# Two tiles of modulation weights for every three projections, instead of one for every two, in a two-layer mLSTM, RWKV-7 and attention trunk

## The chip, the cores and the metric

The kernel runs on one core of a Trainium2 chip. The core has five engines, each with its own queue that is worked off in order: TensorE (PE) for matmuls into PSUM, VectorE (DVE), ScalarE (ACT), GpSimd (POOL), and SyncE (SP), whose queue here does nothing but wait for semaphores and issue DMAs. The metric is the device time of one execution in microseconds (us); lower is better.

## The reference, cut to what matters

Two layers work on 512 latent and 256 context tokens of width 1024. Before each layer a conditioning vector goes through one large matrix (`ada_w`, 1024 x 6144 for each layer), which gives six modulation vectors: shift, scale and gate for the mixer and for the MLP.

```python
def ada_modulation(cond, w, b):
    m = jax.nn.silu(cond) @ w + b
    return jnp.split(m[:, None, :], 6, axis=-1)
...
for layer in range(DEPTH):
    last = layer == DEPTH - 1
    sx1, cx1, gx1, sx2, cx2, gx2 = ada_modulation(c, ada_w[layer], ada_b[layer])
    sc1, cc1, gc1, sc2, cc2, gc2 = ada_modulation(c_ctx[None], ada_w[layer], ada_b[layer])
    nx = modulate(rms_norm(h_lat), sx1, cx1)
    nc = modulate(rms_norm(h_ctx), sc1, cc1)
    if layer % 2 == 0:
        ox, oc = even_mixer(nx, nc, rope, not last, ev_in_w[e], mix_out_w[layer], ml_gate_b[e], ml_norm_w[e],
...
    else:
        ox, oc = odd_mixer(nx, nc, not last, od_in_w[o], mix_out_w[layer], lru_conv_w[o], lru_conv_b[o],
...
    h_lat = h_lat + gx1 * ox
    h_lat = h_lat + gx2 * sq_relu_mlp(modulate(rms_norm(h_lat), sx2, cx2), mlp_w1[layer], mlp_w2[layer])
    if not last:
        h_ctx = h_ctx + gc1 * oc
        h_ctx = h_ctx + gc2 * sq_relu_mlp(modulate(rms_norm(h_ctx), sc2, cc2), mlp_w1[layer], mlp_w2[layer])
return rms_norm(h_lat) * final_norm_w
```

The even mixer projects its input (`in_w`), runs four mLSTM heads in both directions and eight RWKV-7 heads in both directions, each over the context first and then over the latent tokens, and projects the result out.

## The kernel before, in words

**Projections.** All weights are single precision. `split_w` loads one column block of 128 (0.5 MB) through SP, lets ACT round it to `wh`, and lets POOL or DVE form the rest `wl`. `gemm` then multiplies both halves with the split input, 24 matmuls for each segment of tokens: 512 columns for the latent segment (`psg` 128x512), 256 for the context (128x256). Every matmul carries the line number of the helper `mm` (L134).

**Modulation weights.** `ada` is a generator that works on the matrix `ada_w` in parts. A part takes two tiles `adaw` of 2 MB. A tile is two DMAs of 1 MB each on SP's queue, then 32 rows of small matmuls in the trace (16 in the order of the program, where a single-precision matmul is one row), into `psada`: 16 of them need the first DMA, 16 the second. After the second tile of a part, DVE copies `psada` to `rows` (L172), PE transposes that (`pst`, L175) and DVE writes the columns of `mod` (L184). The tile lives in the pool `pa1` with one buffer: the DMA of a tile waits on SP until the matmuls of the tile before it have read it, and everything behind it in SP's queue waits too. Eight parts are worked off in this way in the stretch of which this document speaks, 16 tiles: four parts of layer 0 (the two gates, and the MLP's shift and scale) and four of layer 1 (the mixer's shift and scale, and the gates). None of these values is used in the stretch itself.

**The mLSTM stretch.** A string of tokens sets the order in which Python emits the program. A digit advances that mLSTM head by one projection (`k`, `q`, `v`, output gate, then the head's recurrence over six chunks of 128: `psn`, `pscn`), `c` advances `rwkv_in(0)`, the input side of RWKV-7 for the context. The token `a` starts the draw of modulation tiles: from there each call of `gemm` adds `bg[1]` to a counter, and each time the counter reaches 1 the next tile of `ada` is emitted. From `a` to the end of the stretch there are 26 calls of `gemm`. At the token `R` the rest of `rwkv_in(0)` and then whatever is left of `ada` are emitted. Then the pool `pa1` is closed, its memory goes to the tiles of the RWKV-7 recurrence, and `pre(0)`, the first step's preparation, is emitted. Head 3's last projection and its recurrence are emitted after that.

**What follows.** `pre(s)` loads `bk` and `ar` of step `s` back from DRAM, where `rwkv_in` put them (`bkD`, `arD`, L803 and L804; loads L849 and L850), multiplies them (`psA`), sends a small part through DRAM to POOL, which inverts a triangular matrix in 30 small operations (`Xi`), sends that through DRAM back (`invD`, `Xr`, L895 and L897) and multiplies again (`psI`). Steps 0 to 11 of the recurrence follow, each with `pre` of the next; projections of `rwkv_in(1)` and the layer's other matmuls are drawn in between as filling.

**What sets the order.** A scheduler of the framework takes the emitted program and lays out each engine's queue at build time, from its own estimates of durations. The queue is then fixed: an engine that comes to an instruction whose input isn't there waits, though later ones could run.

Of the kernel before, what the change touches and what calls it, by code (L numbers as in the profile page):

```python
# [117 lines left out]
def hybrid_kernel(ctx: ExitStack, tc: tile.TileContext, A, out):  # L118
# [4 lines left out]
    def nm(s):  # L123
        uid[0] += 1
        return f"{s}_{uid[0]}"
# [6 lines left out]
    def mm(o, l, r, start=True, stop=True, shared=False, tile=None):  # L132
        kw = {"tile_position": (32 * tile[0], 32 * tile[1])} if tile else {}
        return nc.tensor.matmul(o, l, r, start=start, stop=stop, skip_group_check=shared, **kw)  # L134
# [23 lines left out]
    def ada(layer, parts, pa, psa, tag):  # L158
        for pair, half in parts:
            ps = psa.tile([P, 256], F32, tag=tag, name=nm("psada"))  # L160
            for k0 in range(0, NK, 4):

                w = pa.tile([P, 4, D], F32, tag="adaw", name=nm("adaw"))
                for i in range(0, 4, 2):
                    nc.sync.dma_start(w[:, i:i + 2, :], A["ada_w"][layer, pair, half, (k0 + i) // 2])
                for i in range(4):
                    k = k0 + i
                    for j in range(4):
                        mm(ps[32 * j:32 * j + 32, :], sc[:, k, :], w[:, i, 256 * j:256 * j + 256], k == 0, k == NK - 1)
                yield 1.8  # L170
            rows = pa.tile([P, 256], F32, tag="rows", name=nm("rows"), bufs=1)
            nc.vector.tensor_copy(rows, ps)  # L172
            pt = psa.tile([P, 2, P], F32, tag=tag, name=nm("pst"))
            for t in range(2):
                nc.tensor.transpose(pt[:, t, :], rows[:, P * t:P * t + P], ident)  # L175
            src = pt.rearrange("p t (i j r) -> p i t j r", i=2, j=2)
            for i, idx in enumerate(PAIRS[pair]):
                o = 8 * idx + 4 * half
                dst = mod[:, layer, o:o + 4, :].rearrange("p (j t) c -> p t j c", t=2)
                bo = COLS["ada_b"][0] + 48 * layer + o  # L180
                bias = cols[:, bo:bo + 4].rearrange("p (j t) -> p t j", t=2)
                one = 1.0 if idx in (1, 4) else 0.0
                for cnd in range(2):
                    nc.vector.scalar_tensor_tensor(dst[:, :, :, cnd], src[:, i, :, :, cnd], one, bias, op0=ALU.add, op1=ALU.add)  # L184
# [236 lines left out]
    psa1 = st_p1.enter_context(tc.tile_pool(name="psa1", bufs=1, space=PSUM, side="right"))  # L421
# [53 lines left out]
    pa1 = st_a.enter_context(tc.tile_pool(name="pa1", bufs=1))  # L475
# [348 lines left out]
    def add_set():  # L824

        sets.append(st_r.enter_context(tc.tile_pool(name=f"set{len(sets)}", bufs=1)))
# [119 lines left out]
    def new_x(s):  # L946
        return sets[s % 2].tile([P, 2, 4, 2, 64], F32, tag="X", name=nm("X"))
# [141 lines left out]
    for o in "0000a0c1ccc1cc11c1c22cc2c23c12ccc33cR33":  # L1089
        if o == "a":  # L1090
            bg[:] = [itertools.chain(ada(0, ((1, 0), (1, 1), (2, 0), (2, 1)), pa1, psa1, "ada"),
                                     ada(1, ((0, 0), (0, 1), (1, 0), (1, 1)), pa1, psa1, "ada")), 0.5, 0.0]
        elif o == "R":
            for _ in itertools.chain(work["c"], bg[0]):
                pass
            bg[1] = 0
            st_a.close()
            YA[0] = st_y.enter_context(tc.tile_pool(name="py", bufs=1)).tile([P, 4, 4, 64], F32, name="ya_c")
            pr = st_r.enter_context(tc.tile_pool(name="pr", bufs=1))
            add_set()  # L1100
            banks.update(A=(psh2, "h", 1), I=(psa1, "ada", 1))
            S = sets[0].tile([P, 2, 4, 64], F32, tag="S", name="S0")
            nc.vector.memset(S, 0.0)
            X = new_x(0)
            nc.vector.memset(X[0:64], 0.0)
            pre(0, X)
        else:
            next(work[o], None)
# [376 lines left out]
```

## Time and profile before

| | us |
|---|---|
| median of 3 runs | 2063.24 |
| lowest and highest run | 2058.32, 2063.85 |
| the profiled execution, its own time | 2061.51 |
| its span, first to last instruction | 2059.7 |

The sums below are made against the profiled execution: its own time is 1.81 us longer than its span and 1.73 us below the median of the runs. The profile of this execution shows for each engine when an instruction began and how long it took, and for an instruction that waited what released it, in brackets. PE's ends are modelled, since matmuls overlap: what a row of matmuls costs is read from its start to the start of the next. PEclk is TensorE's granted clock as a share of full speed: 1.00 in a stretch means 2.4 GHz throughout, a matmul that takes nearly twice as long as its neighbours ran at the lower level of 1.2 GHz.

### The profile page before, as it was taken

What the parts mean: (1) busy time and instruction counts of PE and PEld (TensorE: products, weight loads), DVE (VectorE), ACT (ScalarE), POOL (GpSimd) and SP (SyncE); (2) the same over time, 40 slices, a digit from 0 to 9 for tenths busy, and PEclk for the clock granted to TensorE, in tenths of its full rate; (3) what the DMA queues carried; (4) which work ended last, traced back from release to release, by engine and by line L of the source; (5) the groups of instructions that cost most, each with busy time, mean ns of one, the idle gap of its engine ahead of it and who ended that gap; (6) DMA issues with size and microseconds to landing.
All of it is one profiled execution on the core that took longest, in us unless ns stands there. A gap on an engine that the chain in (4) does not pass through costs nothing. (4 is left out here: it accounts for less than half of the span.)

```text
span 2059.7 us, 36771 instructions
## 1 busy us (share of the span) xinstructions
PE 1952.0 (95%) x14924; PEld 1604.6 (78%) x14924; DVE 1055.2 (51%) x1944; ACT 875.5 (43%) x1441; POOL 872.4 (42%) x706
## 2 busy tenths in 40 slices
PE   6899998899887999999999999999999999999998
PEld 4788886777677888988787888888666678888887
DVE  6774645676767666766642221353666664122222
ACT  4444444455534443443432332443655654233232
POOL 1455555445534222223244444435444453444444
PEclk9999999999888999999999999999999999999999
DMA  7356557454585555543533323234211122323332
GB/s 301 107 200 214 178 206 262 122 156 124 153 233 143 159 158 156 142 136 124 190 115 125 102 92 103 88 108 153 62 52 34 57 75 82 102 92 101 94 97 78
DMA packets 171833, 271.62 MB, mean 132 GB/s; under 512 B 74960, under 2 KB 113488, under 8 KB 166544
## 3 DMA queue, kind: packets, MB, share of 16 engines
q1 hardware_dynamic: 166608, 263.76, 40.7%
q10 hardware_dynamic: 5056, 5.51, 0.8%
q8 instruction: 118, 1.93, 0.4%
q14 instruction: 51, 0.42, 0.1%
HBM read 244.06 MB, written 25.17 MB: 131 GB/s over the span
## 5 line engine op out<-in xcount | busy, mean ns | idle before, releaser
L241 POOL TENSOR_TENSOR wl<-w,wh 128x1024 fp32r<-128x1024 f32 (+3 forms) x245 | 555.1, 2268 | 829.1 <-PE psg L134 451.9
L237 ACT CAST wh<-w 128x1024 fp32r<-128x1024 f32 (+3 forms) x319 | 313.5, 985 | 543.5 <-PE psg L134 465.1
L134 PE MATMUL psg<-xh,wh 128*128 128x512 f32 (+1 forms) x1440 | 498.2, 361 | 12.8 <-DVE k L710 3.1
L134 PE MATMUL psg<-xl,wh 128*128 128x512 f32 (+1 forms) x1440 | 497.9, 358 | 0.5 <-DVE xl L335 0.4
L134 PEld LDWEIGHTS psg<-xh,wh 128*128 128x128 f32 x1440 | 273.2, 191 | 68.0 <-issue 16.9
L134 PE MATMUL psg<-xh,wl 128*128 128x512 f32 (+1 forms) x1440 | 325.3, 356 | 0.0
L134 PEld LDWEIGHTS psg<-xl,wh 128*128 128x128 f32 x1440 | 275.4, 191 | 45.0 <-issue 7.2
L134 PEld LDWEIGHTS psg<-xh,wl 128*128 128x128 f32 x1440 | 241.9, 190 | 42.1 <-issue 7.3
L134 PE MATMUL psg<-hh,wh 128*128 128x512 f32 (+1 forms) x800 | 266.9, 350 | 6.2 <-DVE r L383 3.2
L134 PE MATMUL psg<-hl,wh 128*128 128x512 f32 (+1 forms) x800 | 268.8, 350 | 0.9 <-DVE hl L281 0.8
L338 DVE SCALAR_TENSOR_TENSOR res_l<-psg,mod,res_l 128x512 f32<-128x512 f32 (+1 forms) x108 | 74.2, 689 | 276.3 <-PE psg L134 276.2
L134 PEld LDWEIGHTS psg<-hh,wh 128*128 128x128 f32 x800 | 151.9, 190 | 27.6 <-issue 4.2
L134 PEld LDWEIGHTS psg<-hl,wh 128*128 128x128 f32 x800 | 152.1, 190 | 20.6 <-DVE hl L281 1.2
L134 PE MATMUL psg<-hh,wl 128*128 128x512 f32 (+1 forms) x800 | 166.4, 350 | 0.0
L134 PEld LDWEIGHTS psg<-hh,wl 128*128 128x128 f32 x800 | 132.9, 191 | 19.2
L383 DVE TENSOR_SCALAR r<-psg 128x512 f32<-128x512 f32 (+1 forms) x96 | 57.4, 600 | 171.4 <-PE psg L134 171.2
L281 DVE TENSOR_TENSOR hl<-r,hh 128x512 fp32r<-128x512 f32 (+1 forms) x96 | 86.8, 907 | 80.4 <-ACT hh L280 80.4
L384 ACT ACTIVATE r<-r 128x512 f32<-128x512 f32 (+1 forms) x96 | 53.5, 560 | 125.8 <-DVE r L383 125.8
L241 DVE TENSOR_TENSOR wl<-w,wh 128x1024 fp32r<-128x1024 f32 (+1 forms) x74 | 88.1, 1191 | 34.9 <-ACT wh L237 15.5
L134 PE MATMUL psada<-adaw,sc 128*32 128x256 f32 (+1 forms) x896 | 62.4, 383 | 7.7 <-DMA adaw<-in_ada_w_dram 4.1
L134 PE MATMUL psA<-ar,bk 64*128 64x128 f32 x384 | 51.5, 295 | 7.3 <-issue 3.0
L280 ACT CAST hh<-r 128x512 fp32r<-128x512 f32 (+1 forms) x96 | 52.6, 550 | 2.8
(422 smaller groups left out, 2900.5 us busy)
## 6 DMA issues: line engine op xcount, KB each, us to landing
w<-in_w_dram SPq DMA_DIRECT2D x192, 512.0 KB, 3.5
adaw<-in_ada_w_dram SPq DMA_DIRECT2D x40, 1024.0 KB, 7.5
w<-in_ev_in_dram SPq DMA_DIRECT2D x47, 512.0 KB, 3.5
w<-in_od_in_dram SPq DMA_DIRECT2D x32, 512.0 KB, 3.5
adaw<-in_ada_dram SPq DMA_DIRECT2D x16, 512.0 KB, 10.8
w<-in_out_w_dram SPq DMA_DIRECT2D x32, 256.0 KB, 2.9
bk<-bkD SPq DMA_DIRECT2D x12, 512.0 KB, 4.7
ar<-arD SPq DMA_DIRECT2D x12, 512.0 KB, 5.7
```

The lines of the kernel that those rows point to most:

```text
L134: return nc.tensor.matmul(o, l, r, start=start, stop=stop, skip_group_check=shared, **kw)
L237: nc.scalar.copy(wh, w)
L241: eng.tensor_tensor(wl, w, wh.bitcast(F32), op=ALU.subtract)
L280: nc.scalar.copy(h, x)
L281: nc.vector.tensor_tensor(l, x, h.bitcast(F32), op=ALU.subtract)
L338: nc.vector.scalar_tensor_tensor(r_, ps, modcol(layer, idx, m, cnd), r_, op0=ALU.mult, op1=ALU.add)
L383: nc.vector.tensor_scalar(r_, ps, 0.0, None, op0=ALU.max)
L384: nc.scalar.activation(r_, r_, AF.Square)
```

## The change

The counter's step goes from 0.5 to 0.67. Nothing else in the program text differs.

```diff
     for o in "0000a0c1ccc1cc11c1c22cc2c23c12ccc33cR33":
         if o == "a":
             bg[:] = [itertools.chain(ada(0, ((1, 0), (1, 1), (2, 0), (2, 1)), pa1, psa1, "ada"),
-                                     ada(1, ((0, 0), (0, 1), (1, 0), (1, 1)), pa1, psa1, "ada")), 0.5, 0.0]
+                                     ada(1, ((0, 0), (0, 1), (1, 0), (1, 1)), pa1, psa1, "ada")), 0.67, 0.0]
         elif o == "R":
             for _ in itertools.chain(work["c"], bg[0]):
                 pass
```

With 26 calls of `gemm`, 0.5 draws 13 times: 13 tiles are emitted between projections, and at `R` three tiles and the last part's transposes are left. With 0.67 it draws 17 times: all 16 tiles and the last part's transposes are emitted before `R`. The pattern is one projection, two, one, two between draws, where it was always two. The scheduler then lays out the queues anew. Counted in the order of the program, the rows of PE are the same in kind and number; those from the second tile of the stretch to the end of the RWKV-7 recurrence stand in a new order. From the MLP of layer 0 on the order is the same but for a few rows.

The first place is SP's queue at the end of the stretch, where the last modulation tiles stood ahead of the loads of `pre(0)`. Before (`adaw_3605` is the last tile, `w_...` a projection's weights, `bk_3649` and `ar_3648` the first loads of `pre(0)`):

```order
L165 DMA adaw_3605<-in_ada_w_dram 128x2048
L810 DMA vD_580<-vt_3545 128x2x128
L165 DMA adaw_3605<-in_ada_w_dram 128x2048
L235 DMA w_4349<-in_ev_in_dram 128x1024
L803 DMA arD_576<-ar_3529 128x4x128
L804 DMA bkD_578<-bk_3530 128x4x128
L235 DMA w_4391<-in_ev_in_dram 128x1024
L849 DMA bk_3649<-bkD_578 128x1024
L850 DMA ar_3648<-arD_576 128x1024
L852 DMA AS_3651<-arD_576 64x8x64 x2
```

The same place in the changed program:

```order
L810 DMA vD_580<-vt_3621 128x2x128
L235 DMA w_4349<-in_ev_in_dram 128x1024
L803 DMA arD_576<-ar_3605 128x4x128
L804 DMA bkD_578<-bk_3606 128x4x128
L849 DMA bk_3649<-bkD_578 128x1024
L850 DMA ar_3648<-arD_576 128x1024
L852 DMA AS_3651<-arD_576 64x8x64 x2
L855 DMA X_3646<-vD_580 64x512 x2
L235 DMA w_4391<-in_ev_in_dram 128x1024
```

No modulation tile is left there, and the loads of `pre(0)` come directly behind the stores that they read, ahead of `w_4391`.

The second place is PE's queue at the end of head 2, around a modulation tile. Before, a projection of `rwkv_in(0)` (`psg_3369`), a tile (`adaw_3446`, the first of four that follow one another with little in between), and the end of head 2 and of an RWKV-7 group:

```order
L134 MATMUL psg_3369<-xh_89,wl_3367 128x256 x8
L175 MATMUL pst_3438<-cst,rows_3436 128x128 x2
L134 MATMUL psada_3445<-adaw_3446,sc 32x256 x16
L683 MATMUL pst_2943<-cst,hall_2924 128x128 x2
L683 MATMUL pst_2947<-cst,hall_2924 128x128 x4
L134 MATMUL psb_3012<-q_3009,cst 128x256
L134 MATMUL psw_3057<-low_1143,uh_3053 128x256
```

The same place in the changed program (the same projection is `psg_3465`, the tile `adaw_3420` is the last of all 16):

```order
L134 MATMUL psg_3465<-xh_89,wl_3463 128x256 x8
L134 MATMUL psada_3361<-adaw_3420,sc 32x256 x16
L175 MATMUL pst_3534<-cst,rows_3532 128x128 x2
L683 MATMUL pst_3010<-cst,hall_2991 128x128 x2
L683 MATMUL pst_3014<-cst,hall_2991 128x128 x4
L134 MATMUL psb_3089<-q_3086,cst 128x256
L134 MATMUL psw_3153<-low_1143,uh_3149 128x256
```

A modulation tile stands at this place in both, and behind it three more tiles came before, none now; the transposes of `rows` now follow directly on the tile's last matmul.

The third place is PE's queue where `pre(0)` takes back the inverse (`psI`). Before:

```order
L134 MATMUL psg_4397<-xh_84,wh_4393 128x512
L134 MATMUL pst_4332<-cst,sq_4330 128x2
L134 MATMUL psI_3756<-Xr_3752,AB_3652 32x32 x16
L134 MATMUL psI_3756<-Xt_3754,AB_3652 32x32 x16
L134 MATMUL pst_4332<-cst,sq_4330 128x2 x3
L134 MATMUL psg_4397<-xl_85,wh_4393 128x512
```

In the changed program:

```order
L134 MATMUL psg_4355<-xl_85,wh_4351 128x512
L134 MATMUL psg_4355<-xh_84,wl_4353 128x512 x5
L134 MATMUL psI_3756<-Xr_3752,AB_3652 32x32 x16
L134 MATMUL psI_3756<-Xt_3754,AB_3652 32x32 x16
L134 MATMUL pst_4332<-cst,sq_4330 128x2 x4
L134 MATMUL psg_4355<-xh_84,wl_4353 128x512 x3
```

`psI` moved up by 16 matmuls of 512 columns: 13 of `psg_4397` and three of `psg_4355` now stand behind it. Between the last `psA` of `pre(0)` and this place there were 85 matmuls of 512 columns and 12 of head 3's recurrence; now there are 69 and 18.

## Rows read from the trace of the kernel before

**Rows 1.** Busy time of each engine in four stretches, granted clock, DMA share, GB/s

```profile
111.00:305.00 194.00, 193.33 (x1477) 158.76 (x1476) 105.44 (x225) 82.12 (x167) 107.70 (x89) 1.00 0.58 202
305.00:360.00 55.00, 49.76 (x350) 35.13 (x348) 33.08 (x80) 27.27 (x56) 28.03 (x34) 0.94 0.77 265
360.00:420.00 60.00, 51.45 (x382) 43.22 (x381) 38.06 (x74) 26.54 (x50) 23.20 (x45) 0.91 0.44 120
420.00:950.00 530.00, 485.58 (x6570) 423.78 (x6569) 362.81 (x776) 243.34 (x429) 186.76 (x236) 0.93 0.56 156
```

**Rows 2.** The same view for tile psada alone: PE, PEld, DVE

```profile
111.00:305.00 194.00, 28.51 (x374) 11.05 (x374) 2.11 (x5) 1.00 0.58 202
305.00:360.00 55.00, 11.54 (x136) 4.06 (x136) 1.25 (x3) 0.94 0.77 265
```

**Rows 3.** DMA issues from 100 to 360 us: count, KB each, median us to landing

```profile
adaw<-in_ada_w_dram SPq DMA_DIRECT2D x30, 1024.0 KB, 7.6
...
bkD<-bk SPq DMA_DIRECT2D x8, 256.0 KB, 4.7
...
ar<-arD SPq DMA_DIRECT2D x1, 512.0 KB, 6.4
```

**Rows 4.** Timeline of SP's queue, 290 to 400 us

```profile
305.75 0.80 SPq L165 DMA_DIRECT2D adaw<-in_ada_w_dram  x2
...
347.62 0.38 SPq L804 DMA_DIRECT2D bkD<-bk  x1
357.50 0.34 SPq L235 DMA_DIRECT2D w<-in_ev_in_dram  x1
359.36 0.33 SPq L849 DMA_DIRECT2D bk<-bkD  x1
359.75 0.42 SPq L850 DMA_DIRECT2D ar<-arD  x1
```

**Rows 5.** Timeline of PE, 224 us and 307 to 314 us

```profile
224.87 1.07 PE L134 MATMUL psada<-adaw,sc 128*32 128x256 f32 x16 [0.55 <-DMA adaw<-in_ada_w_dram]
...
307.63 1.12 PE L134 MATMUL psg<-xh,wl 128*128 128x256 f32 x8
308.60 0.38 PE L175 MATMUL pst<-cst,rows 128*128 128x128 f32 x2
311.28 1.07 PE L134 MATMUL psada<-adaw,sc 128*32 128x256 f32 x16 [2.31 <-DMA adaw<-in_ada_w_dram]
313.61 1.93 PE L134 MATMUL psada<-adaw,sc 128*32 128x256 f32 x16 [1.26 <-DMA adaw<-in_ada_w_dram]
```

**Rows 6.** Timeline of PE, 366 to 393 us: pre(0) and head 3's recurrence

```profile
366.37 1.13 PE L134 MATMUL psA<-ar,bk 64*128 64x128 f32 x8 [3.00 <-issue]
...
368.98 0.64 PE L134 MATMUL pscn<-vt,kw 128*128 128x129 f32 x2
...
376.37 0.39 PE L134 MATMUL pscn<-vt,kw 128*128 128x129 f32 x2
376.59 0.39 PE L134 MATMUL psn<-vt,e 128*128 128x129 f32 x2
...
377.35 1.16 PE L134 MATMUL psA<-ar,bk 64*128 64x128 f32 x8
...
385.13 0.58 PE L134 MATMUL psg<-xh,wh 128*128 128x512 f32 x1 [2.78 <-DVE dn L664]
...
390.47 1.99 PE L134 MATMUL psg<-xh,wl 128*128 128x512 f32 x8
392.30 0.39 PE L134 MATMUL psg<-xh,wh 128*128 128x512 f32 x1
```

**Rows 7.** Timeline of PE: psI of step 0 and of step 2

```profile
409.02 0.45 PE L134 MATMUL psI<-Xr,AB 32*32 32x32 f32 x32 [0.62 <-DMA Xr<-invD]
...
512.98 0.65 PE L134 MATMUL psI<-Xr,AB 32*32 32x32 f32 x32 [2.95 <-DMA Xr<-invD]
```

**Rows 8.** Busy time of PE alone, granted clock, DMA share, GB/s

```profile
370.00:380.00 10.00, 10.00 (x61) 0.74 0.07 16
```

## Prediction

> **What bounds the kernel now.** I read the busy times by stretch first, then the modulation tiles alone, then the timelines of PE and SP around the end of the mLSTM stretch, and last the view of DMAs. The reader is to see two things in the stretches [rows 1]. From 111 to 305 us PE has 193.33 us of work in 194 and a granted clock of 1.00: no gap is left there, and whatever is added to PE lengthens the stretch by its full cost. From 305 to 420 PE stands idle for 5.24 and 8.55 us, and the clock is 0.94 and 0.91, which loses another 3.3 and 5.4 us. This is the tail, where three tiles are drained, `pre(0)` begins and head 3 runs. The change moves work from the tail, which has slack, into the stretch, which has none; it can gain only what the tail loses to waits and to the lower clock.
>
> **Tiles moved.** In the stretch 374 small matmuls cost 28.51 us, 2.44 us for a tile of 32; in the tail 136 cost 11.54, 2.72 for a tile [rows 2]. Three tiles more in the stretch are +7.3, three fewer in the tail -8.1: together -0.8. Bounds: 0, if a tile costs the same everywhere, and -1.5, if the stretch's 0.67 us of gaps takes part of them.
>
> **Landing in the stretch.** A tile's DMA is issued when the last tile has been read, so a tile needs enough other PE work between. Where a wait is seen, a tile issued at 305.75 was used at 311.28, 5.5 us later, and its second half at 313.61, 7.9 later [rows 4, 5]. In the new order the least work between two tiles of the stretch is 36 matmuls of 256 columns; eight of these take 0.97 us from start to start [rows 5], so 4.4 us, and 1.1 of waiting. The next nearest have 5.9, 6.6, 7.1 and 7.2 us of work by the same count: no wait at 5.5. The old wait of 0.55 [rows 5] stood between other tiles and goes. Sum +0.6. Bounds: -0.55, and +6.0, if the first half takes the 7.6 us that is the median of all [rows 3]: then the five places wait 3.2, 1.7, 1.0, 0.5 and 0.4, less the 0.55. The projections' own weights stand behind these DMAs on SP, but the work between the gate and their first use is over 20 us everywhere in the new order, against 4 to 5 for a load.
>
> **The last tile.** Its place behind a projection of `rwkv_in(0)` is like that of a tile that waited 2.31 and 1.26 us [rows 5]. There 24 matmuls and two transposes lay between, now 31 matmuls of 256 columns and two of the recurrence: 4.2 us against 3.2 or so, thus 2.6 of waiting instead of 3.57. But the transposes of `rows` now follow at once, so DVE's copy, 2.11 us for five or 0.42 each [rows 2], is waited for: +0.5. Net -0.5, between -1.0 and 0. The drain's first wait does not go away, it only changes its tile.
>
> A rule of the Trainium skill prices this otherwise. "DMA: Bandwidth & Descriptors", in the section on the anatomy of one DMA, fits a transfer as about 2.0 us plus its bytes at 436 GB/s (measured there for DMAs issued from GpSimd). By an estimate from that page the first megabyte lands after 4.4 us and the second after 6.8, so the stretch would wait nowhere and the last tile 1.6 us, and the sum below would be near -4. The trace disagrees: 5.5 and 7.9 us [rows 4, 5], and the measurement decides.
>
> **The loads of `pre(0)`.** Before, they were issued at 359.36 and 359.75, behind `w` at 357.50 and behind the last tile's transposes, which held the memory; `ar` lands 6.4 us later, at 366.15, and `psA` started at 366.37 after 3.00 us of waiting [rows 3, 4, 6]. The store that they read went out at 347.62 and lands in 4.7: 352.3. In the new order they stand directly behind the stores, so they can go some 7 us earlier. PE comes there earlier too: one tile (2.7) and three rows of the recurrence (0.7) less lie between. Of the 3.00 I leave 0.5: -2.5, between -3.0 and 0 (another store, `arD`, lands late).
>
> **The clock behind that wait.** After the 3.00 us matmuls took 0.64 us that take 0.39 a little later, the lower of the two levels [rows 6], and in 370 to 380 the clock is 0.74 though PE is never idle [rows 8]: 2.6 us lost there alone. Of the 5.4 us lost from 360 to 420 the rest falls to the edges and to the wait of 2.78 us before 385.13 [rows 6], which stays, as it follows head 3's last rows through DVE. A wait of 0.55 left the tile behind it at 1.07 us, full speed [rows 5]. So -3.0, between -3.7 and 0.
>
> **The next wait: `psI`.** From the last `psA` of `pre(0)`, which ends at 378.5, the inverse comes back after 30.5 us, at 409.02, where PE has waited 0.62 us [rows 6, 7]: PE's other work just covers it. In the new order 16 matmuls of 512 columns fewer lie between and six of the recurrence more. Eight of the former take 1.83 us from start to start, one of the latter 0.22 [rows 6]: -3.7 + 1.3, 2.3 us of cover lost. The chain itself (to DRAM, POOL's 30 operations, to DRAM and back) is not shortened by the change, so the wait grows to 2.9: +2.3. That is the length of the wait of step 2, 2.95 us, behind which `psI` took 0.65 us instead of 0.45 [rows 7], so the clock falls here as well: +2.0, less than the 2.6 above. Bounds of both: 0, if POOL's loop is less interrupted, and +5.
>
> **The recurrence.** From 420 to 950 us PE's order is laid out anew, with the same work at the same price; the whole stretch loses 44 us to idle time and some 37 to the clock of 0.93 [rows 1]. By count of matmuls `psI` loses cover at steps 2 and 3 (about 3 and 1.4 us) and gains it at steps 4 and 6 (2.3 and 1.1). I take 0, and a tenth of what is lost there, 8 us either way, as bounds.
>
> **Sum.** -0.8 + 0.6 - 0.5 - 2.5 - 3.0 + 2.3 + 2.0 + 0 = -1.9 us. The profiled execution took 2061.51 us itself, the median of the runs is 1.73 above it: 2059.6 there, 2061.3 as a median. 0.3%, or 6.2 us, is about what a measurement of this kernel can tell from no change.
>
> **Rivals.** *The tail's gain comes through whole.* If the inverse comes back in time for `psI` in its new place, the last two costs fall away and -6.2 is left; with the waits at their lower ends, -9. Middle: -7.5, 2055.7. For it speaks that the scheduler put `psI` there expecting it; against it, that PE already waited 0.62 us with more cover [rows 7], so the expectation was short before.
>
> *Slower: the recurrence waits for its inverses.* Step 2 waited 2.95 us already [rows 7] and has no slack: the 3 us of cover that it loses are waited for in full, step 3's 1.4 likewise, and each puts PE at the lower level for some 2.2 us more. That is +8.8 on top of -1.9: 2070.1. It decides from the point where the inverse of step 2 comes no earlier in relation to its `psA` than before. Against it: steps 4 and 6 get cover back, and work taken from in front of `psI` still has to be done behind it, where it can fill another gap.
>
> *Slower: tiles land late in the stretch.* With 7.6 us for the first half, +6.0 instead of +0.6, and the clock falls once behind the wait of 3.2 us, +2.6: 2069.3. Against it the 5.5 us where a wait shows it, at a DMA share higher than the stretch's 0.58 [rows 1]; 6 MB more there is some 31 GB/s on 202.
>
> *The change does nothing that counts,* since the drain was covered anyway: the time stays at 2063; this lies within the forecast's own range, 2058 to 2066.
>
> **How the numbers follow.** I give the forecast and the case of no effect 0.52 together, the whole gain 0.27, the recurrence 0.14, the late tiles 0.07. The first is within 0.3% and so "same"; the second is faster by over 0.3%, the last two slower. The range, 2053 to 2071, reaches through the middle of the faster case to that of the slower ones and a little beyond, with one in ten left out on each side for the 8 us of the recurrence.
>
> **What would show it.** In the profile after: the 136 small matmuls of the tail [rows 2] fall to some 32 to 64; the stretch before it ends some 7 us later; one tile with a wait of 2 to 3 us in front of head 2's last transposes; `psA` of `pre(0)` with a wait under 1 us, and recurrence rows at 0.39 us behind it; `psI` of step 0 with a wait near 2.9. The prediction is wrong if `psI` waits under 1 us (then the whole gain stands), if the tiles of the stretch wait 3 us or more in sum, or if the waits for `Xr` from 420 to 950 grow by 4 us or more.

## The result, and the profile after

The changed kernel takes 2073.27 us (median; 2071.57 to 2074.59), the kernel before 2063.55 in the same session: a ratio of 1.0053, with an interval of 1.0035 to 1.0071. That is 9.7 us slower, where 1.9 us less were forecast. The profiled execution has a span of 2072.8 and took 2074.59 itself, the longest of the four.

The view of stretches of the kernel after, all engines left out but PE (length, busy time of PE, granted clock, DMA share, GB/s), answers to [rows 1]:

```profile
111.00:305.00 194.00, 191.51 (x1491) 1.00 0.66 232
305.00:360.00 55.00, 47.72 (x301) 0.84 0.46 148
360.00:420.00 60.00, 49.92 (x300) 0.84 0.45 120
420.00:950.00 530.00, 480.51 (x6494) 0.94 0.54 153
```

The same view of the tile `psada` alone answers to [rows 2]:

```profile
111.00:305.00 194.00, 32.29 (x446) 12.43 (x443) 2.93 (x7) 1.00 0.66 232
305.00:360.00 55.00, 6.17 (x64) 2.17 (x64) 0.38 (x1) 0.84 0.46 148
```

As forecast, tiles went from the tail into the stretch: 446 small matmuls for 374 ahead of 305 us, 64 for 136 behind it. But the tail's clock did not rise. It fell, from 0.94 and 0.91 to 0.84 in both parts.

The timeline of PE at the end of the stretch, after; it answers to [rows 5]:

```profile
319.26 1.07 PE L134 MATMUL psada<-adaw,sc 128*32 128x256 f32 x16 [0.87 <-DMA adaw<-in_ada_w_dram]
323.02 1.94 PE L134 MATMUL psada<-adaw,sc 128*32 128x256 f32 x16 [2.68 <-DMA adaw<-in_ada_w_dram]
325.51 0.69 PE L175 MATMUL pst<-cst,rows 128*128 128x128 f32 x2 [0.56 <-DVE rows L172]
326.75 1.54 PE L683 MATMUL pst<-cst,hall 128*128 128x128 f32 x6 [0.56 <-POOL hall L678]
...
331.69 0.79 PE L134 MATMUL psw<-low,uh 128*128 128x256 f32 x2 [0.80 <-ACT uh L769]
...
336.09 0.55 PE L134 MATMUL psg<-xh,wh 128*128 128x256 f32 x1 [1.60 <-DVE k L710]
```

The last tile waits 3.55 us in two pieces. Behind it, where the drained tiles lay, PE waits for VectorE's `k`, and up to 341 us the matmuls of 256 columns run at the lower clock (0.42 in place of 0.28 us behind 336 us). The wait for ScalarE's `uh` is not new. Before, it stood ahead of the first drained tile, no wait for `k` followed, and 256 columns took 0.28 us again behind 325 us. The timeline of PE before:

```profile
320.08 0.50 PE L134 MATMUL psw<-low,uh 128*128 128x256 f32 x2 [1.48 <-ACT uh L769]
...
321.76 1.94 PE L134 MATMUL psada<-adaw,sc 128*32 128x256 f32 x16
...
325.40 0.28 PE L134 MATMUL psg<-xl,wh 128*128 128x256 f32 x1
```

The timeline of PE at `pre(0)`, after; it answers to [rows 6]:

```profile
368.95 1.16 PE L134 MATMUL psA<-ar,bk 64*128 64x128 f32 x8
371.10 0.49 PE L134 MATMUL psn<-vt,e 128*128 128x129 f32 x2 [0.99 <-POOL e L633]
...
374.80 0.80 PE L134 MATMUL psn<-vt,e 128*128 128x129 f32 x2 [1.44 <-POOL e L633]
...
386.87 0.64 PE L134 MATMUL pscn<-vt,kw 128*128 128x129 f32 x2
...
394.42 0.76 PE L134 MATMUL psg<-xh,wh 128*128 128x512 f32 x1 [3.29 <-DVE zs L710]
```

`psA` no longer waits, as forecast. Head 3's recurrence now waits right behind it, 0.99 and 1.44 us for POOL's `e`, and runs at 0.64 us for a row of two matmuls from 375 to 387 us.

The timeline of PE at step 0's `psI`, after, which answers to [rows 7]:

```profile
413.94 0.45 PE L134 MATMUL psI<-Xr,AB 32*32 32x32 f32 x32 [0.60 <-DMA Xr<-invD]
...
417.88 1.35 PE L134 MATMUL pst<-cst,sq 128*128 128x2 f32 x7 [3.01 <-ACT sq L735]
```

`psI` waits 0.60 us, not 2.9. The wait stands one place behind it: the sums of key squares (`pst<-cst,sq`, emitted in `rwkv_in`) follow directly and wait 3.01 us for ScalarE. Before, two of the eight stood ahead of `psI`, six behind it, and none waited.

**The loss by stages.** Fixed times shift, so from here on I measure between instructions that every version has: the transposes of `hall` at the end of heads 0, 2 and 3 (H0, H2, H3), the first `psC<-r` of steps 0 and 3 (C0, C3), and the norm sums `psbc<-cst,rs` behind step 11 (N). The view of stretches between H0, H2, H3, C0, C3 and N, after, PE alone:

```profile
143.83:326.75 182.92, 175.77 (x1346) 0.99 0.63 220
326.75:406.08 79.33, 70.79 (x342) 0.81 0.44 123
406.08:448.66 42.58, 38.43 (x371) 0.92 0.36 103
448.66:594.28 145.62, 130.34 (x1493) 0.91 0.56 159
594.28:1019.38 425.10, 384.50 (x5314) 0.96 0.53 152
```

The same stretches of the kernel before:

```profile
145.40:315.48 170.08, 165.96 (x1246) 0.99 0.61 211
315.48:399.00 83.52, 74.96 (x451) 0.91 0.63 199
399.00:434.86 35.86, 34.18 (x367) 1.00 0.34 100
434.86:585.93 151.07, 136.55 (x1514) 0.89 0.55 158
585.93:1004.40 418.47, 382.24 (x5294) 0.95 0.54 153
```

In this pair H2 comes 11.3 us later, the tail H2 to H3 gives back only 4.2, H3 to C0 costs 6.7, C0 to C3 gives 5.4, and C3 to N costs 6.6. One profile of each is not enough for such differences; four of the runs below have one of these two orders up to C3, and show how far they hold.

### The profile page after: what moved, and what is told of

The parts are those of the page before. It is cut to its first block, busy times and chain, and to the rows that moved or that the text cites. A ratio compares the mean times of both kernels' runs of the same rounds, so it can differ in the third digit from the quotient of the medians.

```text
span 2072.8 us, 36772 instructions
## 1 busy us (share of the span) xinstructions
PE 1954.8 (94%) x14924; PEld 1605.1 (77%) x14924; DVE 1066.0 (51%) x1944; ACT 874.2 (42%) x1441; POOL 862.0 (42%) x706
## 5 line engine op out<-in xcount | busy, mean ns | idle before, releaser
L281 DVE TENSOR_TENSOR hl<-r,hh 128x512 fp32r<-128x512 f32 (+1 forms) x96 | 87.0, 909 | 84.9 <-ACT hh L280 84.7
```

What stands on the lines that cost most here:

```text
L281: nc.vector.tensor_tensor(l, x, h.bitcast(F32), op=ALU.subtract)
```

## The experiments

All changes are against the kernel before or after, as named. Theory A: drained tiles fill waits of the tail, so that little comes back for them. Theory B: tiles drawn more closely land late. Theory C: what follows is laid out in a new order, which wins or loses by itself.

**The number of tiles drawn early.** The step, and once the counter's start, altered in the kernel before:

```diff
-  ... pa1, psa1, "ada")), 0.5, 0.0]
+  ... pa1, psa1, "ada")), 0.5, 0.5]     e1_phase: 13 draws, each one projection earlier
+  ... pa1, psa1, "ada")), 0.58, 0.0]    e2_058: 15 draws
+  ... pa1, psa1, "ada")), 0.42, 0.0]    e4_042: 10 draws
```

> Step 0.5 as before, but the counter starts at 0.5: 13 tiles are drawn as before, each one projection earlier, three are left for the tail. Theory A (the drained tiles filled gaps of the tail, so each tile moved into the stretch costs its 2.4 us and gives nothing back): no tile changes sides, so within 2 us of before. Theory B (the new draws put tiles closer than their DMA needs, and PE waits for landings): the spacing is still two projections, so within 2 us of before. Theory C (the queues are laid out anew, and the recurrence behind them gains or loses by chance): 4 us or more away from before, either way, with the difference behind 420 us.

> Step 0.58: 15 tiles drawn before R, one left for the tail (two tiles more in the stretch than before). Theory A: two thirds of the changed kernel's loss, +5 to +7 us over before. Theory B: some tiles are one projection apart, so part of the loss, +3 to +6. Theory C: no relation to the number, anything from -6 to +12.

> Step 0.42: 10 tiles drawn before R, six left for the tail (three fewer in the stretch). Theory A: faster by up to 7 us if the tail still has gaps to fill, no slower than before. Theory B: the drained tiles follow one another at their landing time in the tail, so slower by 3 to 10 us. Theory C: no relation to the number.

Measured: 2074.6 (ratio 1.0049, 1.0033 to 1.0066), 2069.58 (1.0023, 1.0007 to 1.0039) and 2068.3 (1.0025, 1.0009 to 1.0041). All three are slower, fewer tiles too, and the one that moves no tile into the stretch loses as much as the change. By H3 the profiles differ from before by +0.1, +2.5 and -1.4 us, and by +7.1 for the change; behind it by +10.5, +4.6 and +12.6, without relation to the number of tiles. So in these single profiles the count of tiles orders the time up to H3 and not behind it. The profiled execution of e4 was the slowest of its twelve, 4.4 us above their median, so its 12.6 is too large as a figure for that kernel.

**Landing.** A second buffer for whole tiles did not fit into memory (a later pool wants 31.06 KB for each partition, 17.1 were left), so e3_two_buffers never ran. In its place each tile became two halves in the same memory:

```diff
-                w = pa.tile([P, 4, D], F32, tag="adaw", name=nm("adaw"))
-                for i in range(0, 4, 2):
-                    nc.sync.dma_start(w[:, i:i + 2, :], ...)
+                ws = []
+                for i in range(0, 4, 2):
+                    ws.append(pa.tile([P, 2, D], F32, tag="adaw", bufs=2, name=nm("adaw")))
+                    nc.sync.dma_start(ws[-1], ...)
```

> The change as it is (0.67), but a modulation tile is two tiles of half the size, so that each half's DMA waits only until the same half of the tile before has been read; memory and work are the same. Theory B (tiles land late behind closer draws): the waits of the changed kernel for tiles, 0.48, 1.44 and 3.55 us, shrink together to about 2 or less, the transposes of head 2 come some 3 us earlier than in the changed kernel, and the time falls to 2068 to 2070. Theory A (the drained tiles filled waits of the tail and kept its clock up) and theory C (behind the tail the scheduler lays the order out anew, and what this gives is chance): the waits may shrink, but what comes behind the tail is laid out anew and decides; between 2066 and 2076.

Measured 2072.3 (1.0051, 1.0033 to 1.007): nothing gained. Yet the waits for tiles are gone, as the timeline of PE of this run shows:

```profile
321.49 1.07 PE L134 MATMUL psada<-adaw,sc 128*32 128x256 f32 x16 [0.42 <-DMA adaw<-in_ada_w_dram]
...
326.32 1.54 PE L684 MATMUL pst<-cst,hall 128*128 128x128 f32 x6 [2.78 <-POOL hall L679]
```

Of 5.47 us of such waits 0.42 are left, but head 2's transposes wait 2.78 us for POOL's `hall`. PE needs two things there, and without the first wait it waits for the second: head 2's transposes come at 326.3 us, where they come at 325.9 in the mean without the edit (below). Theory B falls. What head 2's transposes wait for comes up below.

**What drained tiles cost.** Once four of them left out (layer 1's gates, with ones in their place; nothing to drain), once four added to the changed kernel at `R`:

```diff
-                                     ada(1, ((0, 0), (0, 1), (1, 0), (1, 1)), pa1, psa1, "ada")), 0.5, 0.0]
+                                     ada(1, ((0, 0), (0, 1)), pa1, psa1, "ada")), 0.5, 0.0]      e6_no_gates
...
-            for _ in itertools.chain(work["c"], bg[0]):
+            for _ in itertools.chain(work["c"], bg[0], ada(1, ((0, 0), (0, 1)), pa1, psa1, "ada")):   e9_redrain
```

> The kernel before, with two parts of layer 1's modulation, its gates (four tiles), left out and ones in their place: 12 tiles are drawn in the mLSTM stretch, and nothing is left to drain. If drained tiles cost what their matmuls and waits take (8.1 and 3.6 us) and the stretch 2.4 per tile, the transposes of head 3 come 14 us earlier than in the kernel before, and the time is near 2050. Theory A: the three drained tiles fill waits and keep the clock, and so cost about 4 us in place of 11.7; the transposes of head 3 come about 6 us earlier, and with no change behind them the time is 2057. Theory C adds 5 to 13 us behind the transposes of head 3, whatever stands ahead: 2062 to 2070.

> The change as it is, and four tiles of layer 1 (two parts) are read and multiplied a second time at R, with the same results: four tiles are drained again, and all else is as in the changed kernel. If drained tiles cost their matmuls and waits, four are 10.9 us of matmuls and 2 to 4 of waits: head 3's transposes come 13 to 15 us later than in the changed kernel. Theory A: the granted clock between head 2's and head 3's transposes goes back from 0.81 to 0.88 or more, and the four tiles cost 5 to 8 us there. Theory C says nothing of this stretch; behind it the time may differ by some 5 us either way from the changed kernel's: 2076 to 2088 in all.

e6: 2051.13 (0.9942, 0.9921 to 0.9963), 12 us less; at H3 it is 5.7 us early, not 14, and behind H3 it gains 4.9 more, against theory C's expectation that a new order loses. Its tail from H2 to H3, with three drained tiles fewer than before, takes 77.2 us in place of 83.5. e9: 2084.49 (1.0103, 1.0084 to 1.0123). Its tail, in the view of stretches (H2 to H3):

```profile
326.13:412.71 86.58, 81.12 (x471) 0.83 0.63 200
```

Four tiles lengthen the tail from a mean of 78.6 us (four profiles of the same order without them, below) to 86.6: 2.0 us each, not the 2.72 of [rows 2]. The waits of 0.80, 1.60, 0.99 and 1.44 us are filled but for 0.19, that of 3.29 falls to 0.88. So far theory A. But new waits stand there, 1.17 us for `cn` at 381 us and 2.93 for `AS` at 386, so that the idle time only falls from 8.5 to 5.5 us, and the clock stays at 0.83, where 0.88 was expected. That the drained tiles as such kept the clock up is not shown.

**One place of the new order.** In the changed kernel the sums behind `psI` are tied behind the sixth matmul of the projection that follows (`hist` lists the matmuls as they are emitted, `after` fixes the order of two of them; the lines that fill `hist` and `sums` are left out here):

```diff
-                inproj(5 + 3 * p, v)
+                inproj(5 + 3 * p, v); [after(i, hist[-19]) for i in sums if (si, p) == (1, 0)]
```

> The change as it is, with one place of PE's order fixed: the sums of the next segment's first key squares, which stand directly behind step 0's first psI and wait there 3.01 us for ScalarE, are put six matmuls into the projection that follows. If the order behind the tail is where the loss comes from (theory C): the wait shrinks below 1 us, the matmuls behind it take 0.39 us in place of 0.63, the stretch from head 3's transposes to step 0's psC shrinks from 42.6 us to 37 to 39, and the time falls to 2068 to 2070, if nothing behind gives it back. If the place is only where a wait for the chain of the inverse shows: psI's next group waits instead, the stretch stays at 42 to 43, and the time at 2073.

Measured 2070.01 (1.0042, 1.0026 to 1.0058). The timeline of PE there:

```profile
411.12 0.45 PE L134 MATMUL psI<-Xr,AB 32*32 32x32 f32 x32
...
411.81 0.96 PE L134 MATMUL psg<-xh,wl 128*128 128x512 f32 x3
...
414.17 1.05 PE L134 MATMUL pst<-cst,sq 128*128 128x2 f32 x8
```

The wait of 3.01 us is gone, and H3 to C0 takes 35.81 us, as before the change. The time falls by some 2 us by the ratios, 3 by the medians, and the two intervals overlap, so that the gain as a whole is not clear of noise: C0 to C3, laid out anew, takes 156.0 us in place of 145.6, and C3 to N 415.8 in place of 425.1.

**Other places for the tiles.** Layer 1's gates in the recurrence (e11) or in the MLP (e12); the change with 0.75, where the last tile is drawn earlier (e13), and that with the tie of e10 (e14):

```diff
+        with tc.tile_pool(name="pa2", bufs=1, side="right") as pa2:                    e11_gates_late
+            bg[:] = [ada(1, ((1, 0), (1, 1)), pa2, psh2, "h"), 0.5, 0.0]
             yield from lat_mlstm(RES["l"])
...
-    bg[:] = [ada(1, ((2, 0), (2, 1)), pa3, psa3, "ada"), 0.25, 0.0]
+    bg[:] = [ada(1, ((1, 0), (1, 1), (2, 0), (2, 1)), pa3, psa3, "ada"), 0.25, 0.0]     e12_gates_mlp
...
-  ... pa1, psa1, "ada")), 0.67, 0.0]
+  ... pa1, psa1, "ada")), 0.75, 0.0]                                                    e13_075, e14_075_pin
```

> The step of 0.5, and the four tiles of layer 1's gates are drawn not in the mLSTM stretch but in the recurrence, between the output projections of the second segment's mLSTM half, where PE waits much (15.8 us idle between step 3 and the first norm sums in the kernel before); nothing is left out, and nothing is left to drain at R. The kernel without these four tiles ran 12 us faster than before. If tiles cost what their stretch lets them cost (theory A): here 4 to 7 us in all, and the time is 2055 to 2059. If a tile costs its 2.4 to 2.7 us wherever it stands, and its landing waits besides: 2061 to 2064. Theory C: the order behind is laid out anew, 5 us either way.

> The step of 0.5, and the four tiles of layer 1's gates are drawn in the MLP of layer 0, together with the four that are drawn there already, at the same step of 0.25; nothing is left out, and nothing is left to drain at R. PE has no gap there and a granted clock of 1.00, so four tiles cost 2.44 us each, as in the mLSTM stretch: 9.8 us above the kernel without them, 2060 to 2062. Up to the MLP the trace is that of the kernel without them: head 3's transposes some 6 us earlier than before. Should the MLP have cover after all, 2053 to 2057.

> The change with a step of 0.75 in place of 0.67: the same number of tiles in the mLSTM stretch, nothing to drain, but the last one is drawn three projections earlier and no longer waited for in front of head 2's transposes. If the waits for the last tile (0.87 and 2.68 us) are what sends the clock down in the tail: head 2's transposes come 3 to 4 us earlier than in the changed kernel, the clock of the 20 us behind them is 0.9 or more in place of 0.68, and head 3's transposes come 6 to 10 us earlier, near those of the kernel before; the time is 2064 to 2068. If the tail waits for other engines (ScalarE's uh, VectorE's k) whatever stands ahead of it: the wait only moves, the clock falls as before, head 3's transposes come within 2 us of the changed kernel's, and the time stays at 2071 to 2075.

> The step of 0.75 and, besides, the key squares' sums put six matmuls into the projection behind step 0's first psI. Against the step of 0.75 alone: the stretch from head 3's transposes to step 0's psC 5 to 7 us shorter, if the wait of 3 us stands there in it too, the time 1 to 4 us less, as with the step of 0.67: 2061 to 2066 if the last tile's wait was the cause in the tail, 2068 to 2072 if not.

e11: 2088.11 (1.0121, 1.0094 to 1.0147). PE's idle time there is no free place: between 566 and 610 us the DMA share is 0.98, and a projection waits 5.31 us for its input; how much of the 24 us either makes was not taken apart. e12: 2062.03 (0.9981, 0.9965 to 0.9997), close to its expectation: four tiles lengthen what follows the recurrence by 11 us, 2.8 each, and before it the trace is 8.6 us ahead of the kernel before.

e13: 2059.83 (0.9978, 0.996 to 0.9996), the fastest complete version, if by little. But not for the reason given. The timeline of PE:

```profile
328.60 1.54 PE L683 MATMUL pst<-cst,hall 128*128 128x128 f32 x6 [8.58 <-POOL hall L678]
...
333.53 0.79 PE L134 MATMUL psw<-low,uh 128*128 128x256 f32 x2 [0.80 <-ACT uh L769]
...
337.93 0.55 PE L134 MATMUL psg<-xh,wh 128*128 128x256 f32 x1 [1.60 <-DVE k L710]
```

With no tile in front of head 2's transposes PE waits 8.58 us there for `hall`, and then as long for `uh` and `k` as in the changed kernel; the clock falls as in the changed kernel (0.81 from H2 to H3), and H3 is 7.8 us late. What e13 wins over the change stands behind it, from H3 on, with the same tiles drawn and none left:

```profile
406.75:446.40 39.65, 37.14 (x367) 0.91 0.39 104
446.40:593.91 147.51, 133.07 (x1516) 0.92 0.56 155
593.91:1001.66 407.75, 376.71 (x5292) 0.96 0.57 158
```

C3 to N takes 407.8 us, 17 less than after the change. e14 differs from e13 by one tie, shortens H3 to C0 by 1.8 us and loses 12.7 from C3 to N: 2071.96 (1.0031, 1.0015 to 1.0047). In e10 the same tie gained 2 to 3 us, if anything.

**The order alone.** One number of the filling behind the steps from 3 on, with no tile moved; up to C3 the order stays that of the kernel it is made in:

```diff
-    PL = [18, 15, 21, 10, 21]
+    PL = [18, 15, 21, 10, 20]     or 22, in the kernel after (e15) and before (e16)
```

> The change as it is, with one number of the filling altered: from step 3 on, 20 us of other work are pulled in behind a step in place of 21. The mLSTM stretch, the tail and steps 0 to 2 keep the changed kernel's order word for word, so head 3's transposes stay 4 to 7 us later than before. If the loss behind them lies in this order's waits for the inverses (3.54, 3.33 and 2.54 us at steps 5 to 7, 14.1 us in sum in place of 7.2): another order of steps 3 to 11 moves that sum and with it the time, by 4 us or more either way: 2062 to 2069, or 2077 and more. If the loss behind the tail has to do with the tiles: within 3 us of the changed kernel, 2070 to 2076.

> As with 20 us, but 22 in place of 21. Another order of steps 3 to 11: 2062 to 2069, or 2077 and more, if the order decides; 2070 to 2076 if the tiles do. The sum of the waits for the inverses and the time should move the same way.

> The kernel before, tiles untouched, with 20 us in place of 21: the control. If an order laid out anew costs by itself, since the numbers of the kernel before were fitted to its order: 4 to 15 us slower than before, 2067 to 2078, with no tile moved. If the order is a chance that gains as often as it loses: some 5 us either way. If only the tiles count: 2061 to 2067.

> The kernel before with 22 us in place of 21: the second half of the control. 2067 to 2078 if a new order costs by itself, 5 us either way if it is chance, 2061 to 2067 if only the tiles count.

| | ratio | interval | C3 to N, us | waits for `Xr`, 420 to 950, us |
|---|---|---|---|---|
| e15_pl20 | 1.0070 | 1.0045 to 1.0095 | 423.0 | 11.1 |
| e15_pl22 | 1.0065 | 1.0040 to 1.0091 | 420.0 | 6.4 |
| e16_before_pl20 | 1.0043 | 1.0026 to 1.0060 | 420.3 | 13.0 |
| e16_before_pl22 | 1.0025 | 1.0002 to 1.0047 | 433.4 | 12.9 |
| before | 1 | | 418.5 | 7.2 |
| after | 1.0053 | 1.0035 to 1.0071 | 425.1 | 14.1 |
| e13_075 | 0.9978 | 0.9960 to 0.9996 | 407.8 | 6.7 |
| e12_gates_mlp | 0.9981 | 0.9965 to 0.9997 | 407.2 | 11.8 |
| e10_pin | 1.0042 | 1.0026 to 1.0058 | 415.8 | 6.8 |

The medians of the first four are 2080.39, 2081.55, 2073.63 and 2071.51 us, that of the kernel before in the same session 2063.97. With no tile moved, a new order alone costs the kernel before 5 to 9 us by the ratios. That e15 is slower than the change itself is not clear of noise. C3 to N takes 407 to 433 us for the same work; each value is one profile, and executions of one kernel differ too (the seven of e15_pl20 took 2070.87 to 2087.82 us), so a part of this spread is not the order's. The waits for `Xr` do not carry this: they are as long in e12 as in the controls, and short in e10 and e15_pl22.

Four profiles now have the changed kernel's order up to H3 (after, e10, both e15), three of them up to C3; three have that of before (before, both e16). Their means, us:

| | before | after | difference | single values after |
|---|---|---|---|---|
| start to H2 | 315.5 | 325.9 | +10.4 | 326.8, 325.6, 327.4, 323.9 |
| H2 to H3 | 84.7 | 78.6 | -6.1 | 79.3, 77.4, 80.2, 77.4 |
| H3 to C0 | 35.9 | 42.2 | +6.3 | 42.6, 42.0, 42.1 |
| C0 to C3 | 150.7 | 147.7 | -3.0 | 145.6, 148.5, 148.9 |

That is +7.6 us at C3. The other 2 of the 9.7 lie behind it, by difference only.

## Why the prediction was wrong

The rival at 2070.1 us, "the recurrence waits for its inverses", came near the time by luck. Its sign held: the waits for `Xr` grew by 6.9 us, beyond the 4 that I had set. But they grew at steps 5 to 7 (3.54, 3.33, 2.54 us). At step 2, where the rival wanted 3 us more, the wait fell from 2.95 to 0.46, and the table shows that these waits do not decide. Another sign came without what it was to mean: `psI` waits under 1 us, and the whole gain does not stand.

By stages the forecast was +7.4 us up to H2, -13.6 from H2 to H3, +4.3 from H3 to C0 and 0 behind. The last table has +10.4, -6.1 and +6.3, and about -1 behind C0. So the tail makes 7.5 of the 11.6 us between forecast and result. By the prediction's own steps:

- **Tiles moved, in the stretch: nearly right.** H2 was to come 7.4 us later (+7.3 for three tiles, +0.6, -0.5) and comes 10.4 later. In the means, 9.7 of it are there at head 2's last recurrence row: 104 small matmuls more stand ahead of it (7.9 us at 2.44 a tile), and 1.6 us more of waits. Behind that row two things stand at one place, the last tile's waits and `hall`; the prediction has the first alone. In the four profiles of the changed order H2 waits 0.2 to 0.6 us for `hall` when the tile is done. `hall` is ready 11.7 us behind the row; before, it was ready after 9.3, and PE came 1.3 to 2.1 us later still. DVE's addition for `hall` makes the difference. The timelines of DVE and POOL, after and then before:

```profile
319.52 2.92 DVE L671 TENSOR_TENSOR hall<-hall,hs 128x768 f32<-128x768 f32 x1
...
319.01 2.62 POOL L241 TENSOR_TENSOR wl<-w,wh 128x1024 fp32r<-128x1024 f32 x1 [2.60 <-ACT wh L237]
...
308.95 0.96 DVE L671 TENSOR_TENSOR hall<-hall,hs 128x768 f32<-128x768 f32 x1
...
309.01 3.12 POOL L241 TENSOR_TENSOR wl<-w,wh 128x1024 fp32r<-128x1024 f32 x1 [0.98 <-ACT wh L237]
```

In the eight profiles of this document in which POOL was at work when this addition began, it took 2.9 to 3.2 us; in the nine in which POOL was idle at its start, 0.96. No run tests it by itself.

- **Landing and the last tile: too small by 2.4 us, but of no consequence.** The waits up to H2 are 6.6 us in sum now (0.48, 1.44, 3.55, 0.56 and 0.56) against 4.1 before; +0.1 was forecast. (The upper bound of the landing adds up to 6.25, not 6.0.) The last tile's halves were used 5.2 and 8.9 us after the issue at 314.09 (5.5 and 7.9 in [rows 4, 5]); SP took 2.08 us for the two issues here, 0.80 there. By the section that the prediction cites of the Trainium skill's "DMA: Bandwidth & Descriptors" an estimate was 4.4 and 6.8; the trace disagrees again. e3b took the waits away and gained nothing, for in its order `hall` is ready no earlier.
- **The tail: the step that failed.** Three tiles out (-8.1), "The loads of `pre(0)`" (-2.5) and "The clock behind that wait" (-3.0) were to shorten H2 to H3 by 13.6 us; it is 6.1 shorter. The three terms were added as if PE's work and that one wait set the tail's length. In part it is set by chains through POOL, DVE and ACT (`hall`, `uh`, `k`, `e`, `zs`), and the tiles and the loads' wait lay in their gaps. The wait of 3.00 us did go, and others took its place. In the first pair of profiles PE waits 8.6 us from H2 to H3 before (1.48 for `uh`, 3.00 for the loads, 2.78 for `dn`, 1.10 for `hall`, 0.20) and 8.5 after (0.80 for `uh`, 1.60 for `k`, 0.99 and 1.44 for `e`, 3.29 for `zs`, twice 0.2). Over the profiles of the last table the mean idle time (length less busy time) is 10.3 us, 9.6 before, and the mean loss to the clock (length times what the granted clock lacks of 1) 12.0, 7.6 before: +0.7 and +4.4 instead of -2.5 and -3.0. What drained tiles are worth, with all that goes with them, two other comparisons show: four more lengthen the tail by 8.0 us (e9), and three fewer shorten it by 5.5 (77.2, 79.9 and 80.7 us in e6, e11 and e12, which have one order up to H3, against the 84.7). So three drained tiles, with the loads and the clock behind them, are worth 5.5 to 6.1 us and not 13.6. The price of 2.72 us a tile was too high besides: 40 of the 136 matmuls of [rows 2] lie ahead of H2, and the three drained tiles take 7.4 us from start to start. Why the clock fell stays open: from H2 to H3 it is 0.81 to 0.87 in the runs with nothing drained, 0.88 to 0.94 in those of before's order, e1, e2 and e4, which drain one to six tiles, but 0.83 in e9 with four.
- **`psI`: the place wrong, the size near.** Forecast +4.3 (a wait of 2.9 and the clock behind it), measured +6.3, from the wait of 3.01 directly behind `psI`; the wait of `psI` itself stayed at 0.60. The cover that it was to lose is 1.2 us and not 2.3, as six rows of the recurrence behind the last `psA` ran at the lower clock (0.64 us a row), and the chain took 29.3 us in place of 30.5 (from 384.63 to 413.94). e10 shows the place: the wait taken away, the stretch is back at 35.8.
- **"I take 0" for the recurrence: near here, but a mean of a wide spread, and treated as narrow.** With this work at this price, the profiles differ by 26 us from C3 to N, and one tie moves the median by 12 us (e14 against e13), so the bound of 8 either way was too small. Before's order is one of the better ones: of the twelve other versions run here in which the same 16 tiles are drawn up to `R` or drained there, eleven are slower.

So the cause, as far as the runs show it: what the change puts into the stretch costs its full price and 2 to 3 us of waits besides; what it takes out of the tail comes back only in part; and the order behind is a new one, which loses 6.3 us at one place from H3 to C0, gains 3.0 by C3 and loses the rest later. Why one order of the recurrence is better than another stays open; the one place that I could name and undo (e10) was paid back in part elsewhere, and in e14 more than in full.

## What to carry to other kernels

Work that is drained at a stage's end is priced by what the stage waits for when it is gone: run the stage without it before you count its busy time as gain. Where a scheduler lays out queues at build time, an edit comes with a new order of everything behind it; run two or three edits that move nothing but the order, and take the spread of their medians as the bound for that term. If the spread is larger than the edit's own effect, try neighbours of the edit as well (0.75 was 13 us faster than 0.67 by the medians, with the same tiles) and claim no mechanism for the difference.

## What the hardware showed besides

The same order does not meet the same clock in every execution. In the changed kernel's tail the four profiles fall into two kinds. The timeline of PE of e10, to be read beside that of the kernel after:

```profile
369.97 0.55 PE L134 MATMUL psn<-vt,e 128*128 128x129 f32 x2 [0.99 <-POOL e L633]
...
371.31 2.08 PE L134 MATMUL psA<-ar,bk 64*128 64x128 f32 x8
...
373.97 0.80 PE L134 MATMUL psn<-vt,e 128*128 128x129 f32 x2 [0.59 <-POOL e L633]
...
378.81 0.39 PE L134 MATMUL psn<-vt,e 128*128 128x129 f32 x2
```

Here, and in e15_pl22, the lower level begins right behind the first wait, and full speed is back at 378 us, some 7 us later. In the kernel after and in e15_pl20 `psA` behind the first wait still takes 1.13 us; the level falls at the second wait, which is 1.44 us there, and stays for 12 us. The tails of these two are 79.3 and 80.2 us long, those of the other two 77.4: 2 to 3 us, for one queue.
